# The second norm's row sums by two wide matmuls with ones as weights, in a decoder block on one core

## The chip, the cores and the metric

The kernel runs on one core of a Trainium2 chip. The metric is device time in microseconds (us) of one execution; the timed runs of the kernel before gave 723.59, 723.68 and 724.77 us, median 723.68. Engines are named as in the profile: PE (matmuls), PEld (its weight loads), DVE (elementwise), ACT (activations and copies), POOL (elementwise and one DMA queue), SP (the main DMA queue).

## The reference, cut to what matters

One decoder layer over 512 positions of 1024 channels. The first half (a gated convolution, sparse attention, merge gates, `w_o`) is untouched. The change sits where the feed-forward half begins:

```python
    x = x + mix @ w_o[l]
    h = rmsnorm(x, norm2_g[l])                # y = x * rsqrt(mean(x*x) + EPS) * g
    gu = h @ w_ffn_in[l]                      # 1024 -> 2 * 2816
    g = causal_dwconv(gu[..., :D_FF], ffn_conv_w[l]) + ffn_conv_b[l]
    x = x + (jax.nn.silu(g) * gu[..., D_FF:]) @ w_ffn_out[l]
```

## The kernel before

Channels lie on partitions and positions along the free axis, so the norm's sum over channels is a sum over partitions and is made by PE. The norm's factor is applied late: the products run on x times the gain, and rows of the factor, repeated on all partitions (`rb_n2`, 128x512), multiply the products afterwards. Every fp32 product is made of three rounded ones: a value v is kept as h (rounded) and l (the rest, `split`: h by ACT, l by DVE), and `dense` adds wh*xh, wh*xl and, with `lo_last`, the wl*xh products at the end.

**The feed-forward loop.** `ff_tiles(f)` runs for f = 0, 2, ..., 20; it makes two tiles of 128 channels, first the gate half (`ff_pair(f, 0, ...)`), then the up half (`ff_pair(f, 1, ...)`). Below, "pair f/n" is one such call. A pair does a 2x2 block product with seven products instead of eight, on sums of the quarters of x (`xf_h`, `xf_l`, seven forms) and of the weights. The products go into four PSUM banks: b1 (in traces and instruction rows p1 with n and f behind it: `p11_4` is b1 of pair 4/1), b26, b37, b45. The weights' forms are a11 and a12 (`wh_s`, `wl_s`: rounded part and rest of the raw block as loaded), s3, s2, s4, s1 (`sh`, `sl`), and a22 (`th`, `tl`). DVE adds the banks up into `c` (gate half, tile `c0`) or `up`, with `sums`; gate tiles are then multiplied by the rows of the norm's factor, go through the convolution and silu (`cv`), and the up half is multiplied by them.

**Weights.** The raw blocks (`wr`, 512 KB each) are loaded by SP into three buffers; a load waits until the readers of the block that was in its buffer are done. Blocks of the down projection (`wr_d`) take the same three buffers. For some blocks the rest l isn't made by DVE: ACT writes -h into the buffer and a DMA of POOL's queue adds the raw block from memory (`lo_by_dma`; the tables `A1_BY_DMA`, with pairs 2/0, 2/1, 4/0 and 4/1, and `A22_BY_DMA` say which; all down blocks but those of the tail).

**The second norm.** The loop over `order` ends each of eight channel tiles of x1 with `x_forms(j)` (forms of x, split) and a square added into `sq2`. Then `row_scales` makes the sums: four fp32 matmuls with 128 positions of `sq2` as weights and two columns of ones, one for each 128 positions (row sums on partitions, one column each), a DVE scaling (`ms`), a power -0.5 on POOL (`r`), four PE transposes of r spread over 128 columns (`as_rows`), and a copy of the bank into `rb_n2` by ACT. In pair 0/0, `held` puts the last T2 product behind the sums, and the last part of the third form's products behind the transposes.

**What sets the order.** The order on each engine is fixed when the program is built: a scheduler places the instructions by dependences, by its own estimates, and by the explicit `behind` edges. So an edit at one place can move instructions of later pairs against each other. Engines run their rows strictly in that order.

Of the kernel before, what the change touches and what calls it, by code (L numbers as in the profile page):

```python
# [42 lines left out]
TOKC = C_G + 24  # L43
# [48 lines left out]
def tile_block(ctx: ExitStack, tc: tile.TileContext, xT, pos, par, par2, w_tok, w_a3, w_gate, w_ao, w_bo, w_o,  # L92
               w_ff, w_dn, c_w1, out):
    nc = tc.nc
# [331 lines left out]

    def as_rows(name, r, pr):

        for t in range(NT):
            rows = nc.tensor.transpose(pr[:, t * P:(t + 1) * P], r[:, t:t + 1].to_broadcast([P, P]), ident)  # L430
        rb = sb.tile([P, S], F32, name=f"rb_{name}", tag="rb")
        nc.scalar.activation(rb, pr, AF.Copy)
        return rb, rows

    def row_scales(total, name, bank_of):
        pr = bank_of(f"pr_{name}")
        for t in range(NT):
            sums = nc.tensor.matmul(pr[:, 2 * t:2 * t + 2], total[:, t * P:(t + 1) * P], ones[:, 0:2],
                                    start=True, stop=True)
        ms = sb.tile([P, NT], F32, name=f"ms_{name}", tag="ms")  # L440
        r = scales(name, (pr[:, 0:2 * NT].rearrange("p (t two) -> p t two", two=2)[:, :, 0], ms))
        return (r, sums) + as_rows(name, r, pr)

    def wide_scales(h, l, name, bank_of, after):
        pr = bank_of(f"pr_{name}")
        behind(nc.tensor.matmul(pr, ones_r, h, start=True, stop=False), after)
        sums = nc.tensor.matmul(pr, ones_r, l, start=False, stop=True)

        pr4 = pr.rearrange("p (t c) -> p t c", c=P)
        nc.vector.tensor_tensor(pr4, pr4, ident[:, None, :].to_broadcast([P, NT, P]), op=ALU.mult)  # L450
        ms = sb.tile([P, NT], F32, name=f"ms_{name}", tag="ms")
        nc.vector.reduce_sum(ms, pr4, axis=AX.X)
        return scales(name, (ms, ms)), sums, pr
# [629 lines left out]
    first_rest(0)  # L1083
    _, sums2, r2b, rows2 = row_scales(sq2, "n2", d_bank)
    mx_ctx.close()
# [21 lines left out]
    def ff_pair(f, n, c, form, held=None):  # L1107
# [5 lines left out]
        def product(acc, wf, x, k0=0, k1=4, held={}):  # L1113
            wh, wl = form[wf]
            dense(acc, [(wh[:, k * P:(k + 1) * P], wl[:, k * P:(k + 1) * P], xf_h[:, k, x], xf_l[:, k, x])
                        for k in range(k0, k1)], first=k0 == 0, last=k1 == 4, held=held, lo_last=True)

        def sums(dst, bank, v):

            nc.vector.tensor_tensor(dst, bank.rearrange("p (a t) -> p a t", a=2), v[:, None, :].to_broadcast([P, 2, TH]),  # L1120
                                    op=ALU.add)

# [6 lines left out]
        if held:  # L1129
# [162 lines left out]
```

## Time and profile before

| | |
|---|---|
| timed runs, us | 723.59, 723.68, 724.77 (median 723.68) |
| the profiled execution, us | 725.49, of which the span from the first to the last instruction is 723.6 |
| granted TensorE clock | 1.000 over the span |
| DVE busy | 575.6 us (80% of the span) |
| ACT busy | 415.3 us (57%) |
| POOL busy | 125.4 us (17%) |

Times in the trace count from the span's start. Matmuls are pipelined: the duration of one is longer than the distance to the next start, so PE's pace is read from start to start. A number in square brackets behind a row is idle time of that engine just before it, with what ended it. The trace leaves buffer numbers out of names: `p` is any of the banks above, `wl_s` any of the rests.

### The profile page before, as it was taken

The numbers are of one execution on the slowest core, as the hardware profiler recorded it, in microseconds if no ns is written. First come the engines' busy times: TensorE is split into PE (matmuls) and PEld (weight loads), VectorE is DVE, ScalarE is ACT, GpSimd is POOL, SyncE is SP. The second block draws the span as 40 slices with busy tenths as digits, with TensorE's granted clock in tenths as the row PEclk, the third lists the DMA queues.
The fourth block names the chain that finished last, engine by engine and source line by source line (L and its number), as shares of the span: only waits on it lengthen the run. The fifth ranks groups of instructions, "written<-read, shape, count | busy, mean of one in ns | idle before, by whom it ended". The sixth has DMA issues, their size and how long they took to land.

```text
span 723.6 us, 11196 instructions
## 1 busy us (share of the span) xinstructions
PE 716.9 (99%) x4275; PEld 637.1 (88%) x4275; DVE 575.6 (80%) x988; ACT 415.3 (57%) x706; POOL 125.4 (17%) x111
## 2 busy tenths in 40 slices
PE   8999999999999999999999999999999999999997
PEld 8999788888888888878889999999999999999986
DVE  7978967587666675887876998998898988989833
ACT  7776555777767767544665665565445554455320
POOL 1122443343343201231002011010000010000000
PEclk9999999999999999999999999999999999999999
DMA  8633552211111211336446476545655556552413
GB/s 292 227 89 115 145 119 79 60 68 58 59 59 59 87 60 59 116 124 210 160 131 161 117 175 152 169 119 131 164 143 127 136 127 154 128 146 88 117 30 116
DMA packets 36804, 88.19 MB, mean 122 GB/s; under 512 B 7440, under 2 KB 10896, under 8 KB 36752
## 3 DMA queue, kind: packets, MB, share of 16 engines
q1 hardware_dynamic: 30672, 74.42, 32.3%
q0 software_dynamic: 5648, 12.58, 10.7%
q8 instruction: 33, 0.54, 0.3%
q10 hardware_dynamic: 432, 0.49, 0.2%
q14 instruction: 19, 0.16, 0.1%
HBM read 85.39 MB, written 2.10 MB: 121 GB/s over the span
## 4 chain that ended last, share of the span: by engine, by line
PE 92%; issue 4%; DMA 2%; POOL 0%; ACT 0%; DVE 0%; SPq 0%; POOLq 0%; DVEq 0%
PE p L147 8%; PE p L143 8%; PE p L140 8%; PE pdn L143 4%; PE pdn L140 4%; PE pg L145 4%; PE pg L140 4%; PE pg L143 4%; PE pdn L147 4%; PE pa L140 3%; PE pa L143 3%; PE pt L792 2%; PE po L143 2%; PE po L140 2%; PE po L147 2%
## 5 line engine op out<-in xcount | busy, mean ns | idle before, releaser
L140 PE MATMUL p<-xf_h,sh 128*128 128x256 f32 x352 | 87.3, 281 | 0.0
L143 PE MATMUL p<-xf_l,sh 128*128 128x256 f32 x352 | 87.2, 281 | 0.0
L140 PEld LDWEIGHTS p<-xf_h,sh 128*128 128x128 f32 x352 | 66.3, 188 | 0.0
L143 PEld LDWEIGHTS p<-xf_l,sh 128*128 128x128 f32 x352 | 66.3, 188 | 0.0
L930 DVE TENSOR_TENSOR sl<-s,sh 128x1024 fp32r<-128x1024 f32 x44 | 53.1, 1214 | 3.9 <-ACT sh L929 3.9
L147 PE MATMUL p<-xf_h,sl 128*128 128x256 f32 x352 | 55.8, 281 | 0.0
L929 ACT ACTIVATE sh<-s 128x1024 fp32r<-128x1024 f32 x44 | 45.6, 1051 | 17.4 <-DVE s L974 13.2
L955 POOL DMA_DIRECT2D wl_d<-in_w_dn_dram x16 | 19.1, 1195 | 207.2 <-ACT wl_d L952 207.2
L143 PE MATMUL pdn<-al,wh_d 128*128 128x512 f32 x134 | 52.6, 393 | 0.0
L140 PE MATMUL pdn<-ah,wh_d 128*128 128x512 f32 x134 | 52.2, 392 | 0.0
L140 PE MATMUL pg<-xg_h,wh_g 128*128 128x512 f32 x128 | 51.0, 399 | 0.0
L145 PE MATMUL pg<-xg_h,wl_g 128*128 128x512 f32 x128 | 50.8, 397 | 0.0
L143 PE MATMUL pg<-xg_l,wh_g 128*128 128x512 f32 x128 | 50.5, 395 | 0.0
L147 PEld LDWEIGHTS p<-xf_h,sl 128*128 128x128 f32 x352 | 47.9, 188 | 0.3
L743 ACT ACTIVATE e<-sc,mx 128x512 f32<-128x512 f32 (+3 forms) x64 | 33.3, 525 | 18.8 <-DVE mx L742 16.4
L140 PE MATMUL p<-xf_h,wh_s 128*128 128x256 f32 x176 | 43.5, 280 | 0.0
L143 PE MATMUL p<-xf_l,wh_s 128*128 128x256 f32 x176 | 43.4, 281 | 0.0
L140 PE MATMUL pa<-xg_h,wh_a 128*128 128x512 f32 x96 | 38.2, 398 | 0.0
L143 PE MATMUL pa<-xg_l,wh_a 128*128 128x512 f32 x96 | 37.9, 395 | 0.0
L796 DVE TENSOR_TENSOR pl<-pt,ph 128x512 fp32r<-128x512 f32 x40 | 27.3, 685 | 10.8 <-ACT ph L795 10.4
L769 ACT ACTIVATE e<-e,sums 128x512 f32<-128x512 f32 (+3 forms) x64 | 30.9, 556 | 7.5 <-DVE sums L719 7.5
L929 ACT ACTIVATE th<-wr_s 128x512 fp32r<-128x512 f32 x20 | 12.6, 630 | 38.7 <-issue 28.3
(361 smaller groups left out, 2133.5 us busy)
## 6 DMA issues: line engine op xcount, KB each, us to landing
wr_s<-in_w_ff_dram SPq DMA_DIRECT2D x44, 512.0 KB, 3.6
wr_d<-in_w_dn_dram SPq DMA_DIRECT2D x22, 512.0 KB, 3.7
wr_g<-in_w_gate_dram SPq DMA_DIRECT2D x16, 512.0 KB, 3.5
wl_d<-in_w_dn_dram POOLq DMA_DIRECT2D x16, 512.0 KB, 7.0
wr_a<-in_w_a_dram SPq DMA_DIRECT2D x12, 512.0 KB, 3.5
wr_t<-in_w_tok_dram SPq DMA_DIRECT2D x10, 524.0 KB, 5.8
wr_o<-in_w_o_dram SPq DMA_DIRECT2D x8, 512.0 KB, 3.7
wr_ao<-in_w_ao_dram SPq DMA_DIRECT2D x4, 512.0 KB, 3.5
```

The source lines that it names most:

```text
L140: m = nc.tensor.matmul(acc, wh, xh, start=first and i == 0, stop=False)
L143: nc.tensor.matmul(acc, wh, xl, start=False, stop=False)
L145: m = nc.tensor.matmul(acc, wl, xh, start=False, stop=last and i == n - 1)
L147: m = nc.tensor.matmul(acc, wl, xh, start=False, stop=last and i == n - 1)
L743: nc.scalar.activation(e[:, i, 0:nk], sc[:, o:o + nk], AF.Exp, bias=mx[:, i], accum_out=sums[:, i])
L769: nc.scalar.activation(v, v, AF.Copy, scale=sums[:, i])
L792: ends["pt"] = nc.tensor.transpose(pt[:, i * P:(i + 1) * P], e[:, i, kt * P:(kt + 1) * P], ident)
L796: m = nc.vector.tensor_sub(pl, pt, ph.bitcast(F32))
L929: m = nc.scalar.activation(h, v, AF.Copy)
L930: nc.vector.tensor_sub(l, v, h.bitcast(F32))
L955: nc.gpsimd.dma_start(view(l), src, accum_op=ALU.add)
```

## The change

The sums are made as the first norm's already are (`wide_scales`): `sq2` is split into a rounded part and a rest (`sq2_hl`, in a buffer of the tag `wl`), two fp32r matmuls of 512 columns with ones as weights put the sums of all positions on every partition of a bank, DVE multiplies the bank by the identity (four blocks of 128), sums along the free axis (`ms`), then scaling, power, transposes and copy as before. The calls move into pair 0/0: the sums stand ahead of the fourth form's first product and behind the third form's last product, the multiplication by the identity behind the first bank sum, and the transposes behind the pair's last product. What `row_scales` did goes.

```diff
-    def row_scales(total, name, bank_of):
-        pr = bank_of(f"pr_{name}")
-        for t in range(NT):
-            sums = nc.tensor.matmul(pr[:, 2 * t:2 * t + 2], total[:, t * P:(t + 1) * P], ones[:, 0:2],
-                                    start=True, stop=True)
...
-    def wide_scales(h, l, name, bank_of, after):
+    def wide_scales(h, l, name, bank_of, after, after_v=None):
         pr = bank_of(f"pr_{name}")
         behind(nc.tensor.matmul(pr, ones_r, h, start=True, stop=False), after)
         sums = nc.tensor.matmul(pr, ones_r, l, start=False, stop=True)
         pr4 = pr.rearrange("p (t c) -> p t c", c=P)
-        nc.vector.tensor_tensor(pr4, pr4, ident[:, None, :].to_broadcast([P, NT, P]), op=ALU.mult)
+        m = nc.vector.tensor_tensor(pr4, pr4, ident[:, None, :].to_broadcast([P, NT, P]), op=ALU.mult)
+        if after_v is not None:
+            behind(m, after_v)
         ms = sb.tile([P, NT], F32, name=f"ms_{name}", tag="ms")
         nc.vector.reduce_sum(ms, pr4, axis=AX.X)
         return scales(name, (ms, ms)), sums, pr
...
     first_rest(0)
-    _, sums2, r2b, rows2 = row_scales(sq2, "n2", d_bank)
+    sq_hl = sb.tile([P, TOKC], F32R, name="sq2_hl", tag="wl", bufs=2)
+    split(sq_hl[:, 0:S], sq_hl[:, S:2 * S], sq2)
...
-            product(b26[:, hi], 2, T2, held={0: held[0]})
-            product(b37[:, hi], 3, T3, 3, 4, held={0: held[1]})
+            product(b26[:, hi], 2, T2)
+            m = product(b37[:, hi], 3, T3, 3, 4)
...
-        sums(c1, b26, p1)
-        product(b37[:, lo], 4, B22)
+        v = sums(c1, b26, p1)
+        product(b37[:, lo], 4, B22, held={0: held[0](m, v)} if held else {})
...
-        product(b45[:, lo], "a22", T4)
+        m = product(b45[:, lo], "a22", T4)
+        if held:
+            held[1](m)
```

**What moves on DVE at the end of the `order` loop.** Of the program's rows on DVE, here are those from the last x forms to the first sums of pair 0/0 (`c0`), with `wl_s1_0` the rest of the raw block of pair 0/1 and `s320_2`, `s410_2` the weights' sums of pair 2/0. Before:

```order
L930 TENSOR_TENSOR wl_s1_0_4001<-wr_s1_00b_3998,wh_s1_0_4000 128x1024
L1063 TENSOR_TENSOR xv3_3803<-xv3_3803 128x256
...
L930 TENSOR_TENSOR xf_l_3506<-xv3_3803,xf_h_3505 128x512
L973 TENSOR_TENSOR s320_2_4119<-wr_s0_20_4110,wr_s0_21_4112 128x512
L978 TENSOR_TENSOR s410_2_4126<-wr_s0_21_4112 128x512
L974 TENSOR_TENSOR s320_2_4119<-wr_s0_21_4112,s320_2_4119 128x512
L423 TENSOR_SCALAR ms_n2_3875<-pr_n2_3870 128x4
L977 TENSOR_TENSOR s410_2_4126<-wr_s0_20_4110,s320_2_4119 128x512
L1120 TENSOR_TENSOR c0_3890<-p260_0_3893,p10_0_3896 128x2x256
```

The same place of the changed kernel:

```order
L925 TENSOR_TENSOR sq2_hl_3870<-sq2_3510,sq2_hl_3870 128x512
L925 TENSOR_TENSOR xf_l_3506<-xv3_3803,xf_h_3505 128x512
L925 TENSOR_TENSOR wl_s1_0_4004<-wr_s1_00b_4001,wh_s1_0_4003 128x1024
L1124 TENSOR_TENSOR c0_3878<-p260_0_3881,p10_0_3884 128x2x256
L443 TENSOR_TENSOR pr_n2_3947<-pr_n2_3947,ident_89 128x512
L1124 TENSOR_TENSOR c0_3878<-p370_0_3882,c0_3878 128x2x256
L447 TENSOR_REDUCE ms_n2_3951<-pr_n2_3947 128x4
L1124 TENSOR_TENSOR c0_3878<-p450_0_3883,c0_3878 128x512
L1154 TENSOR_TENSOR c0_3878<-c0_3878,p450_0_3883 128x256
L423 TENSOR_SCALAR ms_n2_3951<-ms_n2_3951 128x4
L968 TENSOR_TENSOR s320_2_4122<-wr_s0_20_4113,wr_s0_21_4115 128x512
L973 TENSOR_TENSOR s410_2_4129<-wr_s0_21_4115 128x512
```

`wl_s1_0` has moved behind the last x forms, the four sums for pair 2/0 behind the bank sums of pair 0/0, and three instructions are new (the rest of `sq2`, the multiplication, the reduction).

**What moves on PE in pair 4.** These are PE's rows at the meeting of pairs 4/0 and 4/1: `p450_4` is b45 of pair 4/0, `p11_4` and `p261_4` are b1 and b26 of pair 4/1, and `wl_s1_4` is the rest that a DMA of POOL's queue completes. Between the rows shown stand rows of the same bank and weights. Before:

```order
L140 MATMUL p261_4_4565<-xf_h_3505,wh_s1_4_4541 128x256
L140 MATMUL p450_4_4399<-xf_h_3505,sh40_4_4388 128x256
...
L147 MATMUL p450_4_4399<-xf_h_3505,sl40_4_4389 128x256 x4
L140 MATMUL p450_4_4399<-xf_h_3505,th0_4_4392 128x256
...
L147 MATMUL p450_4_4399<-xf_h_3505,tl0_4_4393 128x256 x4
L147 MATMUL p11_4_4564<-xf_h_3505,wl_s1_4_4542 128x256 x4
L143 MATMUL p261_4_4565<-xf_l_3506,wh_s1_4_4541 128x256
```

The same place of the changed kernel:

```order
L143 MATMUL p261_4_4568<-xf_l_3506,wh_s1_4_4544 128x256
L147 MATMUL p11_4_4567<-xf_h_3505,wl_s1_4_4545 128x256 x4
L147 MATMUL p261_4_4568<-xf_h_3505,wl_s1_4_4545 128x256 x4
L140 MATMUL p450_4_4402<-xf_h_3505,sh40_4_4391 128x256
...
L147 MATMUL p450_4_4402<-xf_h_3505,sl40_4_4392 128x256 x4
L140 MATMUL p450_4_4402<-xf_h_3505,th0_4_4395 128x256
...
L147 MATMUL p450_4_4402<-xf_h_3505,tl0_4_4396 128x256 x4
L140 MATMUL p261_4_4568<-xf_h_3505,sh31_4_4552 128x256
```

All 24 matmuls of `p450_4` (8 with `sh40`, 4 with `sl40`, 8 with `th0`, 4 with `tl0`) stood ahead of the first use of `wl_s1_4` and now stand behind it. Of the eight matmuls of `p261_4` with `wh_s1_4`, five stood ahead of that use and three behind it; now all eight stand ahead.

**What SP's loads wait for.** These are SP's rows from the raw blocks of pair 4/0 to the second block of the down projection, with the semaphores that each waits for: a DVE or Activation semaphore stands for the last reader of the block that was in the load's buffer, a DMAHW one for an earlier load. Before:

```order
L935 DMA wr_s0_40_4369<-in_w_ff_dram 128x1024 [waits DMAHW6_49,DVE_49]
L935 DMA wr_s0_41_4371<-in_w_ff_dram 128x1024 [waits DMAHW7_49,DVE_49]
L1178 DMA wr_d00_4501<-in_w_dn_dram 128x2x512 [waits DMAHW0_49,DVE_49]
L935 DMA wr_s1_40_4537<-in_w_ff_dram 128x1024 [waits DMAHW1_49,DVE_49]
L935 DMA wr_s1_41_4539<-in_w_ff_dram 128x1024 [waits DMAHW3_49,Activation_49]
L1178 DMA wr_d02_4663<-in_w_dn_dram 128x2x512 [waits DMAHW2_49,DVE_49]
```

The same place of the changed kernel:

```order
L930 DMA wr_s0_40_4372<-in_w_ff_dram 128x1024 [waits DMAHW6_49,DVE_49]
L930 DMA wr_s0_41_4374<-in_w_ff_dram 128x1024 [waits DMAHW7_49,DVE_49]
L1184 DMA wr_d00_4504<-in_w_dn_dram 128x2x512 [waits DMAHW0_49,DVE_49]
L930 DMA wr_s1_40_4540<-in_w_ff_dram 128x1024 [waits DMAHW3_49,Activation_49]
L930 DMA wr_s1_41_4542<-in_w_ff_dram 128x1024 [waits DMAHW1_49,DVE_49]
L1184 DMA wr_d02_4666<-in_w_dn_dram 128x2x512 [waits DMAHW2_49,DVE_49]
```

The load `wr_s1_40` (first raw block of pair 4/1, from which `wl_s1_4` is made) took the buffer of `wr_s0_40`, freed by DVE's last sum of it (`s410_4`); now it takes the buffer of `wr_d00`, freed by ACT's copy of it (`wh_d00`).

More of the change, by code (lines that the diff above doesn't have):

```diff
@@ L425, in scales, with as_rows @@
         return r
-    def as_rows(name, r, pr):
+    def as_rows(name, r, pr, after=None):
         for t in range(NT):
             rows = nc.tensor.transpose(pr[:, t * P:(t + 1) * P], r[:, t:t + 1].to_broadcast([P, P]), ident)
+            if after is not None:
+                behind(rows, after)
         rb = sb.tile([P, S], F32, name=f"rb_{name}", tag="rb")
@@ L433, in as_rows @@
         return rb, rows
-    def row_scales(total, name, bank_of):
-        pr = bank_of(f"pr_{name}")
-        for t in range(NT):
-            sums = nc.tensor.matmul(pr[:, 2 * t:2 * t + 2], total[:, t * P:(t + 1) * P], ones[:, 0:2],
-                                    start=True, stop=True)
-        ms = sb.tile([P, NT], F32, name=f"ms_{name}", tag="ms")
-        r = scales(name, (pr[:, 0:2 * NT].rearrange("p (t two) -> p t two", two=2)[:, :, 0], ms))
-        return (r, sums) + as_rows(name, r, pr)
-    def wide_scales(h, l, name, bank_of, after):
+    def wide_scales(h, l, name, bank_of, after, after_v=None):
         pr = bank_of(f"pr_{name}")
@@ L1083, in tile_block, with second_sums, second_rows @@
     first_rest(0)
-    _, sums2, r2b, rows2 = row_scales(sq2, "n2", d_bank)
+    sq_hl = sb.tile([P, TOKC], F32R, name="sq2_hl", tag="wl", bufs=2)
+    split(sq_hl[:, 0:S], sq_hl[:, S:2 * S], sq2)
+    norm2 = []
+    def second_sums(after, after_v):
+        norm2.extend(wide_scales(sq_hl[:, 0:S], sq_hl[:, S:2 * S], "n2", d_bank, after, after_v))
+        return norm2[1]
+    def second_rows(after):
+        norm2.append(as_rows("n2", norm2[0], norm2[2], after)[0])
     mx_ctx.close()
@@ L1114, in product @@
             wh, wl = form[wf]
-            dense(acc, [(wh[:, k * P:(k + 1) * P], wl[:, k * P:(k + 1) * P], xf_h[:, k, x], xf_l[:, k, x])
-                        for k in range(k0, k1)], first=k0 == 0, last=k1 == 4, held=held, lo_last=True)
+            return dense(acc, [(wh[:, k * P:(k + 1) * P], wl[:, k * P:(k + 1) * P], xf_h[:, k, x], xf_l[:, k, x])
+                               for k in range(k0, k1)], first=k0 == 0, last=k1 == 4, held=held, lo_last=True)
         def sums(dst, bank, v):
-            nc.vector.tensor_tensor(dst, bank.rearrange("p (a t) -> p a t", a=2), v[:, None, :].to_broadcast([P, 2, TH]),
-                                    op=ALU.add)
+            return nc.vector.tensor_tensor(dst, bank.rearrange("p (a t) -> p a t", a=2),
+                                           v[:, None, :].to_broadcast([P, 2, TH]), op=ALU.add)
         p1 = pw.tile([P, TH], F32, name=f"p1{nm}", tag="p1", bufs=2)
@@ L1151, in ff_tiles @@
         u = u_bufs[f // 2 % NU]
-        r2 = r2b[:, None, :].to_broadcast([P, 2, S])
         c = u[:, :, 2:]
         share(f, 0)
-        ff_pair(f, 0, c, ff_forms(f, 0) if f else first_form[0], None if f else (sums2, rows2))
+        ff_pair(f, 0, c, ff_forms(f, 0) if f else first_form[0], None if f else (second_sums, second_rows))
+        r2 = norm2[3][:, None, :].to_broadcast([P, 2, S])
         nc.vector.tensor_tensor(c, c, r2, op=ALU.mult)
```

## The prediction

> **What bounds the kernel now.** I read the page first, then PE's waits, then PE, DVE, ACT and the DMA issues around the places that the change moves.
>
> ```profile
> PE 716.9 (99%) x4275; PEld 637.1 (88%) x4275; DVE 575.6 (80%) x988; ACT 415.3 (57%) x706; POOL 125.4 (17%) x111
> ```
>
> ```profile
> PE wu L195 <- POOL ones L191: 1.1, 1, 1.1
> PE p L147 <- DMA wl_s<-in_w_ff_dram: 1.0, 1, 1.0
> PE pj_s L240 <- DVE xg_h L292: 0.8, 1, 0.8
> ```
>
> The first fence is the page's row of busy time, the second all of PE's waits. PE is busy 99% of the span and waits three times: twice in the kernel's first microseconds and once, for 1.0 us, for a `wl_s`. So the time is PE's own work plus these waits, and an edit counts only by PE's instructions and by what it does to waits. The third wait lies here, in PE's timeline (start, duration, instruction, idle time before it):
>
> ```profile
> 426.82 0.28 PE L140 MATMUL p<-xf_h,wh_s 128*128 128x256 f32 x1
> ...
> 428.36 0.28 PE L140 MATMUL p<-xf_h,sh 128*128 128x256 f32 x1
> ...
> 430.73 0.63 PE L147 MATMUL p<-xf_h,tl 128*128 128x256 f32 x4
> 432.37 0.75 PE L147 MATMUL p<-xf_h,wl_s 128*128 128x256 f32 x4 [1.01 <-DMA wl_s<-in_w_ff_dram]
> ```
>
> By the program's order these are b1 of pair 4/1 (426.82), b45 of pair 4/0 (from 428.36 to its last four, at 430.73), and the first use of pair 4/1's rest, which POOL's DMA completes. From 428.36 to 430.73 PE starts 20 matmuls of 256 columns: 0.118 us each. The last four end at about 431.2; the data came at 432.3.
>
> **The sums on PE.**
>
> ```profile
> 382.63 0.28 PE L140 MATMUL p<-xf_h,wh_s 128*128 128x256 f32 x1
> 382.75 0.95 PE L438 MATMUL pr_n<-ones,sq 128*128 128x2 f32 x8
> 383.56 0.49 PE L143 MATMUL p<-xf_l,wh_s 128*128 128x256 f32 x2
> ```
>
> ```profile
> 36.84 0.39 PE L447 MATMUL pr_n<-sq_hl,ones 128*128 128x512 f32 x1
> 37.07 0.32 PE L220 MATMUL pj_o<-wh_t,xg_h 128*128 128x348 f32 x1
> ```
>
> The four narrow fp32 matmuls (two passes each, eight rows) take PE from 382.75 to 383.56, 0.81 us. A wide one of the first norm hands PE on after 37.07 - 36.84 = 0.23 us, so two take 0.46. PE gains **0.35 us** here. The transposes are moved, not changed:
>
> ```profile
> 384.49 1.47 POOL L419 TENSOR_TENSOR r_n<-ms_n,mhalf 128x4 f32<-128x4 f32 x1
> ```
>
> ```profile
> 388.26 0.60 PE L430 MATMUL pr_n<-ident,r_n 128*128 128x128 f32 x4
> 388.61 0.36 PE L140 MATMUL p<-xf_h,sh 128*128 128x256 f32 x1
> ```
>
> They cost the same 0.4 us where they stand now, in pair 0/1, which by 0.118 and 0.23 us a matmul is reached at about 393.5. Their input: the last bank sum of pair 0/0 starts on DVE at about 388.8, the scaling ends by 389.9, POOL's power (1.47) by 391.5. Two microseconds are left, so I cost this move at nothing.
>
> **DVE and ACT.** ACT gets a 128x512 copy (the rounded `sq2`), as long as the one of 380.63, ahead of that one; the idle 0.25 and 0.90 us here take most of it, and what follows (382.17) is moved by 0.4 us at most:
>
> ```profile
> 380.63 0.64 ACT L929 ACTIVATE xf_h<-xv 128x512 fp32r<-128x512 f32 x1 [0.25 <-DVE xv L1066]
> 382.17 1.06 ACT L952 ACTIVATE wl_s<-wr_s 128x1024 fp32r<-128x1024 f32 x1 [0.90 <-DVE xf_l L930]
> ```
>
> DVE gets the rest of `sq2`, a multiplication and a reduction, the last two as in the first norm (median and extreme durations in ns):
>
> ```profile
> L450 DVE TENSOR_TENSOR pr_n<-pr_n,ident x1: 698/698/698, 37.4 to 37.4; 128x512 f32<-128x512 f32 x1
> L452 DVE TENSOR_REDUCE ms_n<-pr_n x1: 692/692/692, 38.1 to 38.1; 128x4 f32<-128x512 f32 x1
> ```
>
> ```profile
> 377.77 1.22 DVE L930 TENSOR_TENSOR wl_s<-wr_s_00b,wh_s 128x1024 fp32r<-128x1024 f32 x1
> ...
> 385.62 0.69 DVE L1120 TENSOR_TENSOR c<-p,p 128x512 f32<-128x512 f32 x1 [0.56 <-PE p L147]
> 390.67 1.42 DVE L1120 TENSOR_TENSOR c<-p,c 128x512 f32<-128x512 f32 x2 [4.35 <-PE p L147]
> ...
> 394.93 1.23 DVE L930 TENSOR_TENSOR sl<-s,sh 128x1024 fp32r<-128x1024 f32 x1 [1.62 <-ACT sh L929]
> ```
>
> So DVE does about 2.0 us more, and the order puts later what it did early: the rest at 377.77 goes behind the x forms (to about 384, when the matmuls that still read its buffer are done), the four sums for pair 2/0 (four of 0.69) behind the bank sums. What hides all this are the gaps of 4.35 and 1.62 us, which go: the third form's products of pair 0/0, for which DVE waited until 390.67, now end near 387.5, since they no longer stand behind the transposes. The 2.0 us of new work and the four sums, 4.4 us starting one after another, fill 6.0 us of gaps. If this cover were gone, DVE would run late by up to 2 us, and PE feels that only through the raw blocks' buffers.
>
> Those buffers are the second cost. The rest at 377.77 frees the buffer for the second raw block of pair 2/0; this load leaves SP at about 385.3 in place of 379.02:
>
> ```profile
> 379.02 0.33 SPq L935 DMA_DIRECT2D wr_s<-in_w_ff_dram  x1
> ```
>
> ```profile
> wr_s<-in_w_ff_dram SPq DMA_DIRECT2D x1, 512.0 KB, 6.3
> ```
>
> The second row is the load of 385.17 before, the nearest in time and company: with about 6 us to landing the sums for pair 2/0 start at about 391. Their copies on ACT stand behind two of pair 2/1's first block (landed near 394; four copies of 0.96 us, to 397.7), so DVE makes the rests from 396.8 to 399.1, and PE wants them from 401.4. That holds with 2 us to spare. DVE thus starts its list from 394.93 on 1.9 us late and later waits about 1.3 us for ACT, where two copies of pair 4/0's block now stand ahead of one for pair 2/1; but four rows of 3.5 us in all (a bank sum of `up0`, one of `c0`, and two products of `cv0`) no longer stand between 394.93 and its rest of pair 2/1's a22 (row 411.87 below), which it reaches at about 411.6, where it was before.
>
> **The wait at 432.** Its chain before, with PE's data last:
>
> ```profile
> 411.87 0.68 DVE L930 TENSOR_TENSOR tl<-wr_s,th 128x512 fp32r<-128x512 f32 x1
> ...
> 416.88 0.68 DVE L977 TENSOR_TENSOR s<-wr_s,s 128x512 f32<-128x512 f32 x1
> ```
>
> ```profile
> 412.58 0.38 SPq L1178 DMA_DIRECT2D wr_d<-in_w_dn_dram  x1
> 417.58 0.94 SPq L935 DMA_DIRECT2D wr_s<-in_w_ff_dram  x2
> 423.64 0.38 SPq L1178 DMA_DIRECT2D wr_d<-in_w_dn_dram  x1
> ```
>
> ```profile
> 416.16 1.06 ACT L952 ACTIVATE wl_d<-wr_d 128x1024 fp32r<-128x1024 f32 x1 [0.38 <-DMA wr_d<-in_w_dn_dram]
> 417.13 1.04 ACT L1182 ACTIVATE wh_d<-wr_d 128x1024 fp32r<-128x1024 f32 x1
> ...
> 422.79 1.07 ACT L952 ACTIVATE wl_s<-wr_s 128x1024 fp32r<-128x1024 f32 x1 [1.47 <-DMA wr_s<-in_w_ff_dram]
> ```
>
> ```profile
> 424.15 0.91 POOL L955 DMA_DIRECT2D wl_s<-in_w_ff_dram  x1 [5.42 <-ACT wl_s L952]
> ```
>
> ```profile
> wr_s<-in_w_ff_dram SPq DMA_DIRECT2D x1, 512.0 KB, 5.1
> wl_s<-in_w_ff_dram POOLq DMA_DIRECT2D x1, 512.0 KB, 8.2
> ```
>
> The last fence gives the landing times of the load of 417.58 and of POOL's DMA of 424.15: 424.15 + 8.2 = 432.3, when PE goes on. In the changed kernel the load of pair 4/1's first block follows ACT's copy `wh_d` (ends 418.17) in place of DVE's sum (ends 417.56). With DVE 0.3 us earlier at 411.6, the copy ends at about 417.9, the load lands 5.1 later at 423.0, ACT's negative ends at 424.1, POOL issues at about 424.35, and with 8.2 the data land at **432.5**, 0.2 later than before.
>
> PE comes there much earlier. The 24 matmuls of b45 of pair 4/0 now stand behind this use, three of b26 of pair 4/1 more ahead of it, and the sums save 0.35: 431.2 - 24 x 0.118 + 3 x 0.118 - 0.35 = 428.4. So it waits 432.5 - 428.4 = about 4.1 us in place of 1.0. Nothing can fill that: PE's queue is in order, and `p450_4` behind it has its weights. Put from the landing: PE goes on at 432.6 in place of 432.4, with 24 - 3 = 21 matmuls more behind it, 21 x 0.118 = 2.5 us. The gain of the sums is swallowed, since it only lengthens the wait; so would be any shorter wait between 382 and 428.
>
> Behind it, the later pairs' order is changed too. Walking the rows I find one more place that is late: the first product of pair 6/0, which stands earlier against the down products than before, meets ACT's copy of its weights about 0.3 us before it is done.
>
> **Sum.** Landing +0.2, matmuls behind it +2.5, pair 6/0 +0.3: **+3.0 us**. Against the profiled execution: span 723.6 to 726.6, with the 1.9 us around it 728.5. The runs shown have their median 1.8 under that execution, so I forecast 723.68 + 3.0 = **726.7**.
>
> The unknown is how long POOL's DMA takes. Nearest rows, POOL's DMA for pair 4/0 at 408.85 (alone) and the one at 435.03 (with a load of SP just behind it):
>
> ```profile
> wl_s<-in_w_ff_dram POOLq DMA_DIRECT2D x1, 512.0 KB, 5.7
> ```
>
> ```profile
> wl_d<-in_w_dn_dram POOLq DMA_DIRECT2D x1, 512.0 KB, 9.0
> ```
>
> With 5.7 the data land at 430.0 and the sum is 2.5 lower, +0.5; with 9.0 it is +3.8. I take 8.2, the same transfer, with a load of SP beside it as before (the one of 423.64, which now leaves about 0.7 us behind it instead of 0.5 ahead).
>
> [...]
>
> **Rivals.**
> - *The wait vanishes* (data by 428.4): PE's gain of 0.35 and the old wait of 1.0 both count, with pair 6/0 +0.3: -1.05 us, 722.6; with all waits gone 722.3. It needs the DMA in 4.1 us, under the 5.7 of the quietest row. [...] 0.06.
> - *The DMA is quick* (5.7 to 6.5): 0.5 to 1.3 us more, 724.2 to 725.0. For it: the load beside it now starts behind it. Against: the row of 9.0 has its load behind it, too. 0.18.
> - *DVE runs late* (the cover isn't enough): the loads for pairs 2/0 and 2/1 take 6 to 7 us beside POOL's DMAs, the sums and their copies come a microsecond or two later still, and each microsecond lands in full on the load of 412 and so on the wait: +4.5 to +5.5, 728.2 to 729.2. 0.16.
> - *The sums don't come off PE's path*: had the wide pair to wait for `sq2`'s rest, PE would idle near 385; DVE has it by about 382. It would be swallowed by the wait anyway.
>
> Forecast 0.60 (725.9 to 727.8). Range 723.6 to 729.2, which leaves the vanished wait out and some of the late DVE. This kernel's runs tell about 0.2% (1.45 us) from no change: slower by more than that 0.75, within it 0.19, faster 0.06.
>
> **What would show it.** The two wide matmuls 0.23 us apart at about 385, the transposes near 393.5 without a wait ahead of them; a wait of about 4 us of PE for a DMA of `wl_s` at 428 to 433, `p<-xf_h,wl_s` followed by 24 matmuls of `sh`, `sl`, `th`, `tl`; no other wait of a microsecond. I am wrong if POOL's DMA of pair 4/1 lands before 430, if the load ahead of it leaves SP well before 417.5 or after 419, or if PE waits somewhere behind 440.

## The result and the profile after

The changed kernel takes **730.77 us** (median of six executions, 728.71 to 731.71) against 723.88 of the kernel before (six, 723.59 to 724.77): ratio 1.0086, 95% interval 1.0071 to 1.0102. It is slower by 6.9 us; the forecast was 726.7, with a range to 729.2. The profiled execution took 728.76, its span is 726.8.

The page's row of busy time and all of PE's waits in the changed kernel (what waits for what, us in total, times, longest):

```profile
PE 719.4 (99%) x4269; PEld 639.3 (88%) x4269; DVE 577.4 (79%) x991; ACT 414.8 (57%) x707; POOL 122.7 (17%) x111
```

```profile
PE p L140 <- DVE c L1154: 1.8, 1, 1.8
PE wu L195 <- POOL ones L191: 1.1, 1, 1.1
PE p L147 <- DMA wl_s<-in_w_ff_dram: 0.4, 1, 0.4
PE pj_s L240 <- DVE xg_h L292: 0.2, 1, 0.2
PE p L140 <- ACT wh_s L924: 0.2, 1, 0.2
```

Two things are to be seen. The wait for `wl_s`, on which the forecast put its 4.1 us, is 0.4; in its place stands a wait of 1.8 us for DVE that was not there before. And PE is *busy* 2.5 us longer than before (719.4 against 716.9), though it has less to do.

The edit itself went as worked out. PE's timeline at the sums and at the transposes:

```profile
384.61 0.40 PE L439 MATMUL pr_n<-sq_hl,ones 128*128 128x512 f32 x1
384.84 0.40 PE L440 MATMUL pr_n<-sq_hl,ones 128*128 128x512 f32 x1
385.08 0.28 PE L140 MATMUL p<-xf_h,sh 128*128 128x256 f32 x1
...
393.23 0.60 PE L430 MATMUL pr_n<-ident,r_n 128*128 128x128 f32 x4
393.58 0.36 PE L143 MATMUL p<-xf_l,sh 128*128 128x256 f32 x1
```

The sums hand PE on after 0.23 us each, the transposes stand at 393.23, and neither has a wait ahead. The loss is made later. PE's timeline at the new wait, and PE, DVE, ACT and the clock in four stretches around it (window, its length, busy us of PE, PEld, DVE, ACT, POOL, then the granted clock, DMA share and GB/s):

```profile
416.68 0.64 PE L147 MATMUL p<-xf_h,wl_s 128*128 128x256 f32 x4
419.08 0.36 PE L140 MATMUL p<-xf_h,sh 128*128 128x256 f32 x1 [1.76 <-DVE c L1154]
```

```profile
413.00:417.00 4.00, 4.00 (x36) 4.00 (x35) 3.95 (x7) 1.00 (x3) 0.00 (x0) 1.00 0.68 167
417.00:419.74 2.74, 0.98 (x8) 0.80 (x7) 2.74 (x5) 1.99 (x3) 0.64 (x1) 1.00 0.02 7
419.74:423.15 3.41, 3.41 (x18) 3.41 (x17) 3.34 (x4) 3.41 (x6) 0.58 (x1) 0.50 0.66 158
423.15:427.00 3.85, 3.85 (x34) 3.85 (x34) 3.61 (x5) 3.56 (x5) 0.91 (x1) 1.00 1.07 267
```

The waiting matmul is the first of `p451_2` (b45 of pair 2/1). Its bank was b45 of pair 2/0 before, and DVE's last sum from that bank comes at 418.52 instead of 413.68, where it was done 2.1 us ahead of PE's first use (414.08 and 416.22). Then the third stretch: for 3.41 us the granted clock is 0.50, PE is busy all the time and starts 18 matmuls, where the 4 us of the first held 36. So the wait of 1.76 us is followed by about 1.7 us (half of 3.41) that look like work.

DVE is late because it waited itself. Its timeline, and ACT's at the same time:

```profile
383.74 1.22 DVE L925 TENSOR_TENSOR wl_s<-wr_s_00b,wh_s 128x1024 fp32r<-128x1024 f32 x1 [1.53 <-PE p L147]
...
410.77 1.23 DVE L925 TENSOR_TENSOR sl<-s,sh 128x1024 fp32r<-128x1024 f32 x1 [2.72 <-ACT sh L924]
411.91 0.69 DVE L1124 TENSOR_TENSOR c<-p,p 128x512 f32<-128x512 f32 x1
...
417.92 0.68 DVE L1124 TENSOR_TENSOR c<-p,c 128x512 f32<-128x512 f32 x1
418.52 0.41 DVE L1154 TENSOR_TENSOR c<-c,p 128x256 f32<-128x256 f32 x1
```

```profile
403.69 1.06 ACT L924 ACTIVATE sh<-s 128x1024 fp32r<-128x1024 f32 x1 [1.75 <-DVE s L969]
407.78 1.06 ACT L947 ACTIVATE wl_s<-wr_s 128x1024 fp32r<-128x1024 f32 x1 [3.02 <-DMA wr_s<-in_w_ff_dram]
408.74 1.04 ACT L937 ACTIVATE wh_s<-wr_s 128x1024 fp32r<-128x1024 f32 x1
409.69 1.05 ACT L924 ACTIVATE sh<-s 128x1024 fp32r<-128x1024 f32 x1
```

The `sh` at 409.69 belongs to pair 2/1. DVE finished its input at 405.6 and ACT was idle, but ahead of it in ACT's queue stand two copies of pair 4/0's first block, for which ACT waits 3.02 us until a load lands. DVE waits behind ACT, PE behind DVE: **a load for pair 4 holds up a bank sum of pair 2**. Before, ACT had this `sh` ahead of those copies (405.64 and 407.49). Neither DVE nor the load is late here: before, the input was done at 405.6, too, and the load had landed by 407.49, only 0.3 us sooner. So it is the order of ACT's rows that makes this wait. The bank sum is 4.8 us late: the `sl` ahead of it starts 2.4 us later (408.40 before), and most of the other 2.4 us are rows of DVE that stood ahead of this `sl` before and now stand behind it.

### The profile page after: what moved, and what is told of

It reads as the page before. It is cut to its first block, busy times and chain, and to the rows that moved or that the text cites. A ratio compares the mean times of both kernels' runs of the same rounds, so it can differ in the third digit from the quotient of the medians.

```text
span 726.8 us, 11188 instructions
## 1 busy us (share of the span) xinstructions
PE 719.4 (99%) x4269; PEld 639.3 (88%) x4269; DVE 577.4 (79%) x991; ACT 414.8 (57%) x707; POOL 122.7 (17%) x111
## 4 chain that ended last, share of the span: by engine, by line
PE 92%; issue 4%; DMA 2%; POOL 0%; ACT 0%; DVE 0%; SPq 0%; POOLq 0%; DVEq 0%
PE p L147 8%; PE p L140 8%; PE p L143 8%; PE pdn L143 4%; PE pdn L140 4%; PE pg L145 4%; PE pg L140 4%; PE pg L143 4%; PE pdn L147 4%; PE pa L140 3%; PE pa L143 3%; PE pt L787 2%; PE po L143 2%; PE po L140 2%; PE po L147 2%
## 5 line engine op out<-in xcount | busy, mean ns | idle before, releaser
L147 PE MATMUL pdn<-ah,wl_d 128*128 128x512 f32 x128 | 34.6, 392 | 0.0
```

The source lines that it names most:

```text
L147: m = nc.tensor.matmul(acc, wl, xh, start=False, stop=last and i == n - 1)
```

## The experiments

Each was timed beside the kernel before, on the same chip; the ratios are to that.

**Is it ACT's order?** `act_order` is the changed kernel, with the two copies behind the `sh` of pair 2/1.

```diff
-            l = lo_by_dma(f"s{n}_{f}", raw, w_ff[f, n])
-            nc.scalar.activation(h[:, 0:D], raw[:, 0:D], AF.Copy)
+            late = ends["sh"] if (f, n) == (4, 0) else None
+            l = lo_by_dma(f"s{n}_{f}", raw, w_ff[f, n], after=late)
+            hi = nc.scalar.activation(h[:, 0:D], raw[:, 0:D], AF.Copy)
+            if late is not None:
+                behind(hi, late)
```

> The changed kernel with one thing moved: ACT's two copies of pair 4/0's first block (wl_s0_4, wh_s0_4) are ordered behind its copy sh41_2 of pair 2/1, as before the change; nothing is left out. Theory (ACT's queue: sh41_2 has its input at 405.6 but stands behind copies whose load lands at 407.8, DVE waits 2.7 us for it, its bank sum of pair 2/0 is late, PE waits 1.8 us at p451_2 for the one o bank, and the granted clock then halves for 3.4 us): DVE's gap of 2.7 us ahead of sl41_2 goes, PE's wait at 417 goes, the granted clock stays 1.0 near 420; PE reaches the rest of pair 4/1 at about 428.3 and waits there 1.5 to 4 us; 725 to 728.5 us against 723.9 before and 730.8 changed. Rival (the DVE work that the sums add, or the later sums of pair 2/0, costs the time): the wait at 417 stays at 1.5 us or more and the time at 730 to 731.5. Rival (only the clock matters): 722 to 723.

726.00 us, ratio 1.0036 (1.0019 to 1.0054). In the profiled execution the wait at 417 and the half clock behind it are gone, though the load at the head of the list leaves SP as late as in the changed kernel:

```profile
384.97 0.33 SPq L930 DMA_DIRECT2D wr_s<-in_w_ff_dram  x1
```

```profile
405.80 1.06 ACT L924 ACTIVATE sh<-s 128x1024 fp32r<-128x1024 f32 x1 [0.86 <-DVE s L975]
```

What remains of its waits in this stage:

```profile
PE p L147 <- DMA wl_s<-in_w_ff_dram: 1.4, 1, 1.4
```

So the order of three rows on ACT, with the few rows of DVE and PE that moved along with them, makes 4.8 of the 6.9 us by the medians, and 3.6 by the ratios (1.0086 and 1.0036 of 724). Single executions still range from 724.42 to 732.56 us. It isn't all, and the next link appears: the wait that the forecast spoke of, at 1.4 us, not 4.1.

**Taking that wait out, too.** `both_orders` also puts the `wl_s` products of pair 4/1 behind the 24 matmuls of `p450_4`, as before.

```diff
-        product(b1[:, lo], "a11", B11)
+        product(b1[:, lo], "a11", B11, lo_after=ends["p45"] if (f, n) == (4, 1) else None)
...
-            product(b26[:, lo], "a12", B21)
+            product(b26[:, lo], "a12", B21, lo_after=ends["p45"] if (f, n) == (4, 1) else None)
```

> As the kernel with ACT's order mended, and on PE the rests of pair 4/1 (p11_4 and p261_4 with wl_s1_4) are ordered behind the 24 matmuls of p450_4; nothing is left out. Theory (the change's own work is free, the two places in the order cost all of it): no PE wait at 417, at most 1.2 us at 432, clock 1.0 throughout; 722.0 to 724.5 us, so 6 to 8 us under the changed kernel and not slower than before. Rival (the added DVE work costs): 727 or more. Rival (the order moved again elsewhere): a new PE wait of over 1.5 us and 725 to 728.

727.80 us, 1.0059 (1.0037 to 1.0081): the theory (at most 724.5) missed, and the interval overlaps that of `act_order`. The wait for `wl_s` is gone, and one of 1.2 us for DVE's last sum of `up2` has come:

```profile
PE p L140 <- DVE up L1159: 1.2, 1, 1.2
```

Removing a wait by hand moved the limit to DVE's queue. I followed it two steps further. `three_orders` puts three taps of pair 2's convolution behind that bank sum, `four_orders` two weight sums of pair 4/1 (`s321_4`, `s411_4`) as well:

```diff
+        if f in LATE:
+            late.extend(taps[f % 2:])
...
+        if (f, n) == (4, 1):
+            behind(m1, ends["v"])
+            behind(m2, ends["v"])
```

> As the kernel with both orders mended, and on DVE three of the four convolution steps of cv2 are ordered behind the bank sum of p451_2 (up2), which p450_4's first product waits for; nothing is left out. Theory (DVE has no gap from 397 to 437 and is late there, so that PE meets it at the one o bank): the sum starts at about 425.5 instead of 428.1, the wait of 1.2 us at 428 goes, no wait of over 0.5 us behind 377; 722.3 to 724.3 us, 1.2 us or more under the kernel with two orders mended. Rival (the rests by POOL's DMA are the bound): PE waits 1 us or more for a wl_s or a wh_s instead, and the time stays at 725 to 728.

> As the kernel with three orders mended, and DVE's first two sums of pair 4/1 (s321_4 and s411_4, which wait for the load of its second block) ordered behind the bank sum of p451_2. Nothing is left out. Theory (a bank sum that stands in DVE's queue behind an instruction waiting for a load): the sum starts near 424 to 426 whatever the load takes, the wait of 2.0 us at 428 goes; 723.5 to 725.7 us. Rival (every change of order only moves the wait): another wait of 1 us or more between 400 and 460, 725.7 to 729.

726.95 us (1.0039, 1.0025 to 1.0053) and 726.51 (1.0032, 1.0019 to 1.0044). In the first the wait grew to 2.0 us: the bank sum now stood behind a weight sum that waited 2.7 us for a load. In the second that is gone, and three smaller waits are in its place:

```profile
PE pdn L140 <- ACT ah L926: 0.7, 1, 0.7
PE p L147 <- DVE sl L927: 0.5, 1, 0.5
PE p L140 <- ACT wh_s L926: 0.3, 1, 0.3
```

My theory that each edit would win back its wait missed both times. Behind the first step, mending the order row by row gained nothing that can be told from the noise, so I looked ahead of these rows.

**What does an idle PE cost?** `clock_probe` is the kernel before with a tail that computes nothing of the reference: bursts of 44 matmuls with idles of 0.97 to 1.97 us between them.

```diff
...
+    for i, step in enumerate(steps + steps[::-1]):
+        pd = d_bank(f"probe{i}")[:, 0:TH]
+        for m in range(44):
+            nc.tensor.matmul(pd, w[0][:, 0:P], y[:, 0:TH], start=m == 0, stop=m == 43)
+        nc.vector.tensor_scalar(y[:, 0:TH], pd, 1.0 / 16, None, op0=ALU.mult)
+        for c in step:
+            nc.vector.tensor_scalar(y[:, 0:c], y[:, 0:c].bitcast(F32), 1.0, None, op0=ALU.mult)
```

> The kernel of before with a tail that writes no output: 38 bursts of 44 matmuls (5.2 us each), between them DVE operations of growing, then of falling size, so that PE idles about 1.2 to 3 us each time. Theory (the clock is judged in fixed stretches of 3.41 us, and it is halved for the next stretch where PE idled over about half of one): drops last 3.41 us or a multiple, they begin a multiple of 3.41 us apart, idles under 1.7 us are never followed by one, those between 1.7 and 3.4 us in a part of the cases, by where they fall in the stretch. Rival (a length alone decides, between the 1.01 us that did nothing and the 1.76 us that was followed by a drop): every idle over that length is followed by a drop, at the same distance behind it. Rival (idle time is not the cause): no drops in the tail. Time 723.9 plus about 38 x 7.2 us, so near 1000.

In the tail the clock fell three times, for 3.41 us each, at 836.07, 846.31 and 870.21: 10.24 and 23.90 us apart, 3 and 7 times 3.41, so on one grid in this run. Stretches of that grid (window, length, busy us of PE, clock, DMA share, GB/s):

```profile
825.83:829.24 3.41, 1.70 (x15) 1.00 0.00 0
829.24:832.66 3.42, 3.42 (x31) 1.00 0.00 0
832.66:836.07 3.41, 1.64 (x14) 1.00 0.00 0
836.07:839.48 3.41, 3.41 (x17) 0.50 0.02 5
842.90:846.31 3.41, 1.57 (x13) 1.00 0.01 2
846.31:849.72 3.41, 3.41 (x18) 0.50 0.00 0
849.73:853.14 3.41, 2.13 (x18) 1.00 0.00 0
853.14:856.55 3.41, 2.72 (x22) 1.00 0.00 0
```

An idle of 1.71 us inside one stretch left the next at 1.00, 1.77 and 1.84 halved it (1.84 a second time ahead of 870.21). Idles of up to 1.97 us that a boundary cut in two (the last two rows) left it at 1.00. So in this trace an idle of 1.77 or 1.84 us inside one 3.41-us stretch paid another 1.7 us (half of 3.41) in the next, one of 1.71 us did not, and whether a wait of 1.8 to 2 us paid depended on where the grid fell.

**The same kernels once more.** `after_again` and `after_third` are the changed kernel, `before_again` the kernel before.

> The changed kernel once more, for a second profiled execution. Theory: PE waits at p451_2 for DVE's c0 at 417 again, 1.4 to 2.5 us; whether the clock halves behind it depends on where the wait falls, so the time is 728.5 to 729 without a drop and 730 to 732 with one or two. Rival (the wait and the drop were an accident of one execution): no wait of over 1 us at 417, 726 to 727.

> The changed kernel beside these, timed on the same chip. Theory: PE waits 1.5 to 2.5 us at p451_2 in every execution, and the runs differ by whether the granted clock halves once or more behind it or behind the wait at 432: those at clock 1.0 within 1 us of 728.5, those at 0.998 or less 730 or more. Rival (clock without part in it): times and clocks unrelated.

> The kernel of before once more, for a second profiled execution. Theory (the profile shown first was a long one: its POOL DMA of pair 4/1 took 8.2 us, and its wait of 1.0 us at 432 and 0.85 us at the start are not in the usual execution): the DMA takes 5 to 6.5 us, the wait at 432 is under 0.3 us, span near 722. Rival (the wait is in every execution): 0.8 to 1.2 us at 432 and span 722 to 723.6, with the difference elsewhere.

`after_again` took 728.53 us, with waits of 1.9 us at 417 and 1.5 for `wl_s`, and no half clock behind either. An estimate puts the first across a boundary: in the first profile of the changed kernel the clock fell at 419.74 and again at 726.94, 307.20 us or 90 times 3.413 apart; the same distance back from the half clock at this execution's end (from 725.48 us), the stretch to 418.28 has 1.51 us of it and the next 0.37. `after_third` has 731.48 us (1.0102, 1.0087 to 1.0117), with 728.29 profiled and the others 731.44 to 731.87. Its profiled execution has no wait at 417, and this at 428 (stretches as above, PE, PEld, DVE, ACT, POOL):

```profile
427.56:430.97 3.41, 1.54 (x11) 1.13 (x10) 3.41 (x7) 2.15 (x3) 0.00 (x0) 1.00 0.55 171
430.97:434.38 3.41, 3.29 (x15) 3.32 (x16) 3.41 (x5) 2.34 (x5) 0.00 (x0) 0.50 0.28 74
```

Two short waits, 1.2 us for `wl_s` and 0.8 for `up` (of which 0.1 lies behind the boundary), together leave PE 1.54 us of the first stretch, and the second runs at half clock. So the theory of `after_third` missed in both its parts: the wait at 417 isn't in every execution, and the clock doesn't sort the times (728.29 us at 0.996, the others at 0.997 and 0.998). The changed kernel thus has no single wait of its own: its three traces differ in which queue is late by a microsecond. And `before_again` took 724.74 us (span 722.1). These are all its waits on PE, with POOL's DMA of pair 4/1:

```profile
PE wu L195 <- POOL ones L191: 1.1, 1, 1.1
PE pj_s L220 <- ACT th L171: 0.2, 1, 0.2
```

```profile
421.73 0.91 POOL L955 DMA_DIRECT2D wl_s<-in_w_ff_dram  x1 [4.21 <-ACT wl_s L952]
```

The DMA leaves 2.4 us earlier than in the first profile (424.15), takes 7.1 us where 5 to 6.5 were expected, and PE doesn't wait for it. The 1.0 us of the first profile's third wait was that execution's own.

**Which part of the change?** Three kernels do one part alone: `split_only` is the kernel before with the split of `sq2` into a `wl` buffer, and nobody reads it; `sums_only` has the wide sums at their old place; `moves_only` has the new places with the narrow sums.

```diff
     first_rest(0)
+    sq_hl = sb.tile([P, TOKC], F32R, name="sq2_hl", tag="wl", bufs=2)
+    split(sq_hl[:, 0:S], sq_hl[:, S:2 * S], sq2)
     _, sums2, r2b, rows2 = row_scales(sq2, "n2", d_bank)
```

> The kernel of before with its narrow sums and its places, plus one idle part of the change: sq2 is split into a wl buffer (one copy on ACT, one subtraction on DVE), which nothing reads. Theory (the wl buffer): wl_s1_0's rest and pair 2/0's sums go late as in the changed kernel, DVE runs late, and PE waits 1 us or more for a bank sum or a rest between 400 and 435; 726.5 to 731 us. Rival (the sums' DVE work or the moves): within 0.7 us of before, 723.5 to 724.8.

> The kernel of before with the two wide matmuls, the multiplication and the reduction in place of the four narrow ones, at the old places ahead of b26's products, with sq2_hl in the wl buffer; transposes at their old place; nothing is left out. Theory (the wl buffer): 726 to 731 us, DVE late, a PE wait of over 1 us between 400 and 435. Rival (the moved transposes and products cost it): 722.5 to 724.5. Rival (the order that comes out decides case by case): here ACT's copy sh41_2 stands ahead of those of pair 4/0, so no wait at 417, 723 to 726.

> The changed kernel with the four narrow matmuls of before for the sums, but at the new places (sums behind the third form's products, transposes behind the last); no split of sq2, no wl buffer; nothing is left out. Theory (the wl buffer): 722.5 to 724.7 us, pair 2/0's sums at 382 to 386. Rival (the moves cost it): 726 to 731.

727.04 us (1.0047, 1.0029 to 1.0064), 734.45 (1.0141, 1.0127 to 1.0155) and 728.71 (1.0063, 1.0049 to 1.0077). PE's longest waits behind 377 us, in `sums_only` and in `moves_only`:

```profile
PE p L147 <- DMA wl_s<-in_w_ff_dram: 5.6, 2, 4.1
PE p L140 <- DVE up L1153: 1.0, 1, 1.0
```

```profile
PE p L140 <- ACT wh_s L924: 3.0, 1, 3.0
PE p L147 <- DMA tl<-in_w_ff_dram: 1.7, 1, 1.7
```

Against the 724.29 of the kernel before, timed beside them, the parts cost 2.8, 10.2 and 4.4 us; they don't add up to 6.9, and each waits for something else (`sums_only` also has two stretches at half clock, 434.0 to 440.8). The expectations of `sums_only` and `moves_only` missed. `moves_only` is the one to remember: it has neither the split nor its buffer, its load leaves SP as early as before (378.50 and 379.02), and it is 4.4 us slower all the same. `pinned_free` below has the same moves in the order of before and loses nothing, so the order found anew costs that much here, without any buffer being taken. `split_only`, one copy and one subtraction which nobody reads, has a load 3.7 us later than before (382.67), but its order was found anew as well: on PE its `wl_s` rows of pair 4/1 stand ahead of all 24 matmuls of `p450_4`, as in the changed kernel. Its 2.8 us don't tell the buffer from the order.

**The buffer.** The split's result lies in the ring of two `wl` buffers that the rests of the raw blocks use, until PE has read it. `own_buffer` puts it in an `xv` buffer, and `pinned_order` also holds the order of before on every engine by explicit edges.

```diff
-    sq_hl = sb.tile([P, TOKC], F32R, name="sq2_hl", tag="wl", bufs=2)
+    sq_hl = pv.tile([P, 6, TH], F32R, name="sq2_hl", tag="xv", bufs=2).rearrange("p a c -> p (a c)")
```

> The changed kernel, but the two halves of sq2 (sq2_hl) lie in a buffer of the x forms (tag xv) that is free by then, in place of a wl buffer that pair 1's rest wl_s1_0 waits for; nothing is left out, and the order is found anew. Theory (the wl buffer: it puts wl_s1_0's rest from 377.8 to 383.7, hence the load of pair 2/0's second block from 379 to 385 and its four sums from 382 to 390.8, and DVE stays 2 to 4 us late through 430, where PE meets it at the one o bank): rest back at about 378, the load at about 379, no PE wait at p451_2 or p450_4, the wait for the rest of pair 4/1 under 1.5 us; 722.0 to 724.0 us, clock 1.0 in nearly all runs. Rival (the 2 us of added DVE work, or the moved transposes and products, cost it): 726 to 731.

> The change's arithmetic in the order of before: two wide matmuls with sq2_hl in the x forms' buffer, multiplication and reduction on DVE, sums behind the third form's products and transposes in pair 0/1, but every other instruction from the x forms of the last tile to the end in the order that before has on PE (from pair 2/0 on), DVE, ACT, POOL and SP, by a list of numbers. Nothing is left out. Theory (the order in which loads, copies and bank sums queue costs the time, not the added work): no PE wait over 0.5 us behind 377 us, clock 1.0 in nearly all runs, 722.8 to 724.5 us, so within 0.2% of before. Rival (DVE's 2 us of added work is what PE meets at the bank sums): a wait of 1 us or more for a bank sum between 405 and 435, 725 to 728.

728.22 us (1.0055, 1.0042 to 1.0069) and 726.74 (1.0038, 1.0025 to 1.0050): both theories missed, and in `pinned_order` the rival's sign came, a wait of 1.0 us for a bank sum (`up`, at 405.88). The trace shows that this buffer isn't free either. ACT's first copy of pair 2/0 takes over the memory of that pool, and waits for PE's sums (it runs at 385.3 instead of 382.2). POOL's DMA behind it leaves about 3.1 us later (386.6 and 386.7 instead of 383.5). Of SP's loads beside it, one takes 7.8 us in `own_buffer`, and two take 7.2 and 7.3 in `pinned_order`; in the two profiles of before they take 5.1 to 6.4. So these runs changed one wait for another, and could not tell order from work.

The last pair could. `free_buffer` puts it in a buffer of `ah` (inputs of the down products, first written at 411 us), behind the closing of the earlier pools; `pinned_free` is the same with the order of before held on every engine.

```diff
-    sq_hl = sb.tile([P, TOKC], F32R, name="sq2_hl", tag="wl", bufs=2)
-    split(sq_hl[:, 0:S], sq_hl[:, S:2 * S], sq2)
...
+    sq_hl = pf.tile([P, 2, S], F32R, name="sq2_hl", tag="ah", bufs=NA // 2).rearrange("p a t -> p (a t)")
+    split(sq_hl[:, 0:S], sq_hl[:, S:2 * S], sq2)
```

> The changed kernel with the low half sq2_hl in a buffer of the pool that the branches' stage does not use yet, split after the earlier pools are closed, so that no copy and no load waits for it; the order is found anew by the walk. Theory (the loss is made by the order of the in-order queues and by the buffers, not by the 2 us of work on DVE): the rows behind 377 us still stand where the walk puts them, so one or two waits of 0.3 to 1.5 us stay between 395 and 447 us; 724.5 to 729 us, and the waits of this run name other rows than those of the kernel after. Rival (the work itself costs): a wait of 1 us or more for DVE at a bank sum between 405 and 435 us in this run too, 728 to 731.5 us.

> The same code, with the order of the kernel before held on every engine; what differs from before is one more copy on ACT, five more rows on DVE, and on PE the narrow sums gone, two wide matmuls with ones and the transposes. Theory (order and buffers make the loss): no wait over 0.5 us on PE behind 377 us other than those of before, the narrow sums' 0.35 us gained, the 0.65 us of the down weights' buffer paid only if they lie in the other buffer (matmuls 233 instead of 230 ns apart); 722.8 to 724.5 us. Rival (2 us of work on DVE cost by themselves): a wait of 1 us or more for a bank sum on DVE between 405 and 435 us, 725 to 728 us.

**724.07 us** (1.0002, 0.9993 to 1.0011) and **724.05** (1.0001, 0.9992 to 1.0010) against 724.03 of before: the whole loss is gone. In `free_buffer` this comes with an order found anew, against its theory, which had waits of 0.3 to 1.5 us left. All of PE's waits in `free_buffer`, then in `pinned_free` (whose recorded lines are all L112):

```profile
PE wu L195 <- POOL ones L191: 1.1, 1, 1.1
```

```profile
PE wu L112 <- POOL ones L112: 1.1, 1, 1.1
PE pr_n L112 <- POOL r_n L112: 0.5, 1, 0.5
```

DVE does the same added work there, so the work isn't what costs. `pinned_free` against `pinned_order` is the cleanest pair: the traces have the same work in the same order on every engine, but for the sums' own rows, a few products beside them on PE and one row of DVE, and with the other buffer the time is 2.7 us less (726.74 and 724.05). DVE's rows in `free_buffer`, and the load that follows the first of them:

```profile
377.41 1.22 DVE L925 TENSOR_TENSOR wl_s<-wr_s_00b,wh_s 128x1024 fp32r<-128x1024 f32 x1
...
383.89 0.68 DVE L925 TENSOR_TENSOR sq_hl<-sq,sq_hl 128x512 fp32r<-128x512 f32 x1
```

```profile
378.66 0.33 SPq L930 DMA_DIRECT2D wr_s<-in_w_ff_dram  x1
```

```profile
399.49 1.05 ACT L924 ACTIVATE sh<-s 128x1024 fp32r<-128x1024 f32 x1
...
401.66 1.07 ACT L947 ACTIVATE wl_s<-wr_s 128x1024 fp32r<-128x1024 f32 x1 [0.86 <-DMA wr_s<-in_w_ff_dram]
```

In the changed kernel the rest of pair 0/1 comes at 383.74 instead of 377.41, waiting for PE to leave the buffer, and the load behind it at 385.03 instead of 378.66:

```profile
385.03 0.33 SPq L930 DMA_DIRECT2D wr_s<-in_w_ff_dram  x1
```

It isn't shown that these 6.4 us are the head of the chain to 417: at 405.6 DVE was where it was before, and `act_order` has the same late load without the wait. In `free_buffer` buffer and order differ together: the `sh` of pair 2/1 runs at 399.49, not 409.69, ahead of the copies that wait for the load, and PE has no wait behind it. No run holds the order of before with the `wl` buffer, so what this buffer costs by itself stays open, and so does whether it is the reason for the order that was found.

**The down weights' buffer.** The changed kernel has its down matmuls a little further apart. `wh_flip` is the kernel before with one unused `wh` tile ahead, so that all later ones swap their two buffers.

```diff
+        if name == "t04":
+            none = sb.tile([P, TOKC], F32R, name="wh_none", tag="wh", bufs=2)
+            nc.gpsimd.memset(none[:, 0:2].bitcast(F32), 0.0)
```

> The kernel of before with a memset of two columns in an extra wh tile at the start, so that every wh tile lies in the other one of the two wh buffers; the order is the same on every engine. In all changed kernels so far the down products' wh_d tiles lie in the other buffer than in before, and their matmuls follow one another 233.2 ns apart instead of 230.0. Theory (the buffer sets it): 233 ns here too, and 0.4 to 0.9 us more than before. Rival (it comes with something else): 230 ns and 723.7 to 724.3 us.

724.64 us against 724.02 (1.0007, 0.9998 to 1.0015). The time doesn't settle it; the trace does: from start to start the 268 `pdn<-...,wh_d` matmuls of 512 columns are on average 230.2 ns apart before and 233.1 with the buffers swapped, in the same order on PE and with no other wait. The changed kernel has 232.8; that its `wh_d` lie in the swapped buffer is what the expectation says, and no trace shows it. Over 268 such matmuls that is 268 x 2.6 ns = 0.70 us; the 134 with `wl_d` come 1.2 ns closer, -0.16, which leaves about 0.5 us.

## Why the prediction was wrong, by its own steps

- **The sums and the transposes** were right: 0.23 us a matmul, no wait ahead, transposes at 393.2 (said: 393.5).
- **The three links ahead of ACT** were right: the load at 385.03 (385.3), the sums for pair 2/0 from 390.78 (391), DVE's rests from 396.83 (396.8). I costed them at nothing, because PE wanted the weights only from 401.4. As far as the traces show that held: DVE ended the input of pair 2/1's `sh` at 405.6 in both kernels.
- **"DVE ... later waits about 1.3 us for ACT" and reaches its rest of pair 2/1's a22 "at about 411.6, where it was before": this step failed.** It waited 2.72, and the rest came at 413.24. ACT's copies of pair 4/0's block, which I had seen ahead of the `sh`, were held by a load that landed at 407.75. And I followed this lateness only down the chain to the load of 412, not to the bank sums that stand in the same DVE queue. One of them had 2.1 us to spare before: c's last sum of `p450_2`, for a bank that b45 of pair 2/1 needs. It came 4.8 us later, and PE waited 1.76. `act_order`, which puts the `sh` back ahead of the copies, shows that this order was the cause of that wait.
- **"So would be any shorter wait between 382 and 428" be swallowed: failed.** A wait of 1.76 us was not only a wait; 3.41 us at half clock followed it, which cost PE another 1.7. These 3.5 us, the waits of 0.4 and 0.2 and about 0.5 of the down matmuls make 4.6 of the 4.7 us that the profiled span has over `before_again` (726.8 and 722.1).
- **The wait at 432.** The chain came as walked, later: load at 419.79 (said: 417.9, and after 419 was named as a sign of being wrong), POOL's DMA at 426.05 (424.35), but in 6.0 us instead of 8.2, so the data landed at 432.0 (432.5). PE arrived at 431.65 instead of 428.4, having lost 3.5 us on the way, and waited 0.41. `act_order` shows it without that loss: 1.4 us, the DMA taking 5.5. The 8.2 us was the wrong row to take, the 5.7 the right one (5.7 and 5.8 in `after_again` and `after_third`). At 446.92 PE waited 0.24 for pair 6/0 (said: 0.3).
- **The base.** The profiled execution was put at span 726.6, and came at 726.8. That agreement is chance: the sum had the wrong terms. The step from there to 726.7, which took 1.8 us off, failed. `before_again` shows what most of that 1.8 us was: its span is 1.5 us shorter, and it has neither the third wait nor the one of 0.8 us in the kernel's first microseconds. A profile with waits that the median lacks can't be the base for a change that lengthens those waits.
- **"DVE runs late"**, at 0.16, was the nearest rival. It had DVE late, but for the loads' sake and not by ACT's order, its price at the wrong place, in the wait at 432, and no half clock.

What makes the timed median 2 us longer than the profiled execution isn't shown. The granted clock over the span was 0.995 to 0.998 in the executions of 730 to 732 us, where one stretch at half clock is 0.5 x 3.41 / 727 = 0.0023: one or two such stretches each. But the profiled executions of 728.76 and 728.29 us had 0.998 and 0.996, so the clock doesn't explain the difference, and the waits of the long executions left no trace.

So the change does what it says, and it neither costs nor brings anything that can be measured when its operand lies in a buffer that nobody waits for and the order is a good one: that of before, or the one that `free_buffer` happened to get. `moves_only` shows that an order found anew need not be. The 0.35 us saved on PE doesn't show: in `pinned_free` a wait of 0.5 us for POOL's power stands against it. In `free_buffer` the down matmuls with `wh_d` are 232.2 ns apart instead of 230.2, about 0.5 us in 268. No version beat the kernel before by more than its uncertainty.

## What to carry to other kernels

A new operand in a ring that the loads' buffers turn on came with a load 6.4 us later here: cost such an operand by the rows whose buffer it takes. Where the order is found anew, look for rows that wait for a load and now stand ahead of rows that don't, and follow each late row to *every* reader in the same queue, not only down the chain that was critical before. Where a change alters a built order, try the same work in a buffer that nobody waits for, and with the old order held, before its work is blamed. Take the base of a sum from an execution that has the median's waits.

## What the hardware showed that was not expected

- In `clock_probe` the granted clock stayed at 1.00 behind a 3.41-us stretch with 1.71 us of idle PE, and was 0.50 for the next 3.41 us behind stretches with 1.77 and 1.84. In `after_third` two waits of 1.2 and 0.8 us left PE idle for 1.87 us of one stretch, and the next was at 0.50.
- The same matmuls, in the same order, start 230.2 or 233.1 ns apart by the buffer that their weights lie in (`wh_flip`). With the order of before held it was 230.2 in `pinned_order` and 231.6 in `pinned_free`, where the operand takes a buffer of the ring of `ah`; so the weights' place need not be all of it, and why is open.
- POOL's adding DMA of 512 KB took 5.5 us (`act_order`) to 8.2 (the first profile of before) for the same transfer of pair 4/1. In that profile of before, an SP load of the same size took 3.3 us with none of POOL's under way (379.02), and one took 8.5 us beside a DMA of POOL's (435.70).
